# The gate z of the first layer, projected with channels as rows

## The chip, the core and the metric

The kernel runs on one core of a Trainium2 chip. The metric is the device time of one execution in microseconds (us); lower is better. Five engines work from queues of their own, each in its own order: TensorE (PE, with its weight loads listed as PEld), VectorE (DVE), ScalarE (ACT), GpSimd (POOL) and SyncE (SP, which issues most transfers). An instruction waits at the head of its queue until its semaphores are there, and everything behind it on that engine waits too.

## What is computed

Two mixers follow each other over 1024 tokens of 1024 channels: a gated DeltaNet layer, then a Mamba-2 layer. The change lies in the first one. Cut to what matters:

```python
proj = hid @ w_in
qkv, z, b_raw, a_raw = jnp.split(proj, [...], axis=-1)
qkv = jax.nn.silu(_causal_conv(qkv, conv_w))
...                                   # 8 key heads, 16 value heads of 128
o = _chunk_gated_delta_rule(q, k, v, g, beta).astype(hid.dtype)
o = _rmsnorm(o, norm_w) * jax.nn.silu(z.reshape(b, t, GDN_H_V, GDN_DV))
return o.reshape(b, t, GDN_V_W) @ w_out
```

z is a projection of 2048 channels, silu(z) a factor for each element of the normalised output, and the product goes into the output projection.

## The kernel before

The first layer runs in 8 groups g, each of one key head with its two value heads. In a group, q, k and the two v heads are projected by `proj_halves` (L160): the weights of 128 channels stand in the array, and 512 tokens stream past. One *half* is 24 matmuls 128x512 (L170, L171, L172: three products of high and low parts of a float32, over 8 slices of the 1024 input channels) into one `ps_proj` bank, of which there are two. Each half is drained by the convolution: ACT reads the bank (L202, L205), DVE adds three taps (L209), ACT and DVE make the silu (L189, L190). The weights come by a transfer to `wr`, a cast on ACT to `wh` (L86) and a subtraction on DVE to `wl` (L87); `wh` and `wl` have three slots each, each for half of the input channels.

The gate z is made the other way round, by `z_chunk` (L224): for each 128-token chunk n the tokens are the weights of the array, and 256 columns (two heads) of the z weights stream past, 24 matmuls 128x256 (L232, L233, L234). The result has tokens as rows. ACT takes a tanh (L238), DVE makes the silu (L239). The weights of z (`zh`, `zl`, one set of tiles) are loaded for a whole group by `load_zw` (L215).

The scan of a group walks over the 8 chunks. A *chain step* is a loop through three engines: `KS` on PE (L631, state S times k), `vpp` on DVE (L634), `NV` on PE (L639), `p` on ACT (L642), `dS` on PE (L648), S on DVE (L651, L654), and then the next KS. Beside it, `prep` makes the next chunk's operands (L609 to L620), and `output` makes the chunk's result o (L666, L668), its scale `so` (ACT and POOL, L680 to L683) and yn = o x so x z on DVE (L685). Two steps later `store` turns yn with two transposes on PE (L66) into `ps_tr`, ACT copies that to `yg` with the norm's weight (L695), and SP sends it off to y0d.

The order of the work: the program emits, in each of 8 slots of a group, one piece of scan S, one piece of I (the block inverse of the next group, L466) and one of J (a half of q, v, k of later groups), with z of the chunk inside the scan's piece. The scheduler then orders each engine's queue, the chain going with priority. At the very start the DVE queue is laid out by hand by a string, one letter a piece: Z (load of z's weights), I (inverse of group 0, 31 pairs of L490 and L492 among it), Y (three early z chunks), J, Q.

## Time and profile before

| | us |
|---|---|
| median of 3 runs | 1994.41 (1993.93 to 1996.84) |
| profiled execution: its own time is its span | 1993.9 |
| PE busy | 1918.5 (96%) |
| PE weight loads busy | 1644.6 (82%) |
| DVE busy | 1397.9 (70%) |
| ACT busy | 1120.4 (56%) |
| POOL busy | 420.5 (21%) |

Busy times are sums over the span; shares are of the span. Matmuls overlap, and their ends are modelled, so that two starts in a row tell more than a busy time. In a timeline a row's first number is its start in us from the span's beginning, its second how long it was listed as busy, and a bracket at its end names the idle time ahead of it on its engine and what ended it. x2 or x4 behind a row are so many matmuls that go as one row there: each product of float32 operands in the scan is listed as two.

### The profile page before, as it was taken

To read this page: it belongs to the slowest core of one execution; us is meant where nothing else is said; L and a number is where in the kernel's file an instruction comes from. 1 tells how busy PE (TensorE), PEld (TensorE's weight loads), DVE (VectorE), ACT (ScalarE), POOL (GpSimd) and SP (SyncE) were. 2 spreads that over 40 slices of the span, in tenths; PEclk is the share of its full clock that TensorE was granted. 3 is DMA by queue.
4 is the path that set the end of the run, shared out by engine and by line. 5 is a ranking of instruction groups with operands and counts; after the bars stand their busy time and mean duration, and the time that the engine had idled before them with its cause. 6 is when DMAs were issued, how large, how long until landed. Compare 5 with 4: busy or idle time off the path is not lost.

```text
span 1993.9 us, 36924 instructions
## 1 busy us (share of the span) xinstructions
PE 1918.5 (96%) x13086; PEld 1644.6 (82%) x13086; DVE 1397.9 (70%) x3330; ACT 1120.4 (56%) x3058; POOL 420.5 (21%) x818
## 2 busy tenths in 40 slices
PE   7997999899999999999999999999999999999998
PEld 5776888788888888897878788888888888897886
DVE  6797686777678776844355678778787877878433
ACT  5645656575656656564343466666665656566332
POOL 1201211212122212100000032333333233332000
PEclk9997999999999999999999999999999999999999
DMA  4421423232232423225474232222231322246754
GB/s 140 117 54 51 96 56 83 67 78 75 50 96 47 106 49 104 56 90 164 142 222 140 64 89 82 64 72 78 80 83 55 90 59 70 79 123 184 214 170 141
DMA packets 284796, 193.42 MB, mean 97 GB/s; under 512 B 65425, under 2 KB 246338, under 8 KB 284610
## 3 DMA queue, kind: packets, MB, share of 16 engines
q1 hardware_dynamic: 284610, 191.05, 34.1%
q8 instruction: 103, 1.69, 0.4%
q14 instruction: 83, 0.68, 0.1%
HBM read 159.34 MB, written 31.65 MB: 96 GB/s over the span
## 4 chain that ended last, share of the span: by engine, by line
PE 71%; DMA 8%; DVE 8%; ACT 4%; POOL 2%; issue 2%; SPq 1%; POOLq 0%; DVEq 0%; ACTq 0%
PE ps_proj L170 9%; PE ps_proj L172 8%; PE ps_proj L171 8%; PE ps_proj L352 5%; PE ps_proj L354 5%; PE ps_proj L353 5%; PE ps_proj L232 5%; PE ps_proj L233 5%; PE ps_proj L234 5%; PE ps_tr L66 2%; DMA X<-xd 2%; DVE acc L209 2%; PE ps_sc L910 2%; PE ps_pt L66 2%; PE ps_sc L639 1%
## 5 line engine op out<-in xcount | busy, mean ns | idle before, releaser
L170 PE MATMUL ps_proj<-hid_h,wh 128*128 128x512 f32 x1024 | 413.4, 404 | 5.2 <-ACT acc L205 4.0
L172 PE MATMUL ps_proj<-hid_h,wl 128*128 128x512 f32 x1024 | 404.0, 395 | 0.0
L171 PE MATMUL ps_proj<-hid_l,wh 128*128 128x512 f32 x1024 | 402.0, 393 | 0.0
L232 PE MATMUL ps_proj<-zh,hid_h 128*128 128x256 f32 x1024 | 297.5, 291 | 1.1 <-DVE z L239 1.0
L234 PE MATMUL ps_proj<-zh,hid_l 128*128 128x256 f32 x1024 | 294.7, 288 | 0.0
L233 PE MATMUL ps_proj<-zl,hid_h 128*128 128x256 f32 x1024 | 291.8, 285 | 0.0
L170 PEld LDWEIGHTS ps_proj<-hid_h,wh 128*128 128x128 f32 x1024 | 192.4, 188 | 44.7 <-ACT acc L205 4.9
L172 PEld LDWEIGHTS ps_proj<-hid_h,wl 128*128 128x128 f32 x1024 | 192.3, 188 | 40.6
L171 PEld LDWEIGHTS ps_proj<-hid_l,wh 128*128 128x128 f32 x1024 | 192.7, 188 | 34.8
L352 PE MATMUL ps_proj<-woh,yh 128*128 128x512 f32 x512 | 205.5, 402 | 6.4 <-ACT yh L86 4.0
L353 PE MATMUL ps_proj<-wol,yh 128*128 128x512 f32 x512 | 203.5, 400 | 0.7 <-DVE wol L87 0.7
L354 PE MATMUL ps_proj<-woh,yl 128*128 128x512 f32 x512 | 202.5, 398 | 1.2 <-DVE yl L87 1.0
L232 PEld LDWEIGHTS ps_proj<-zh,hid_h 128*128 128x128 f32 x1024 | 194.9, 190 | 6.5 <-DVE z L239 2.6
L233 PEld LDWEIGHTS ps_proj<-zl,hid_h 128*128 128x128 f32 x1024 | 195.0, 190 | 3.3
L234 PEld LDWEIGHTS ps_proj<-zh,hid_l 128*128 128x128 f32 x1024 | 195.0, 190 | 0.3
L209 DVE SCALAR_TENSOR_TENSOR acc<-raw,cw_ssd,acc 128x512 f32<-128x512 f32 x192 | 150.6, 785 | 19.4 <-ACT acc L207 17.2
L86 ACT CAST yh<-yr 128x512 fp32r<-128x512 f32 x128 | 79.0, 619 | 140.7 <-PE ps_proj L353 86.2
L87 DVE TENSOR_TENSOR yl<-yr,yh 128x512 fp32r<-128x512 f32 x128 | 88.7, 694 | 95.5 <-ACT yh L86 93.8
L209 DVE SCALAR_TENSOR_TENSOR acc<-raw,cw_gdn,acc 128x512 f32<-128x512 f32 x192 | 145.4, 758 | 12.6 <-ACT acc L205 11.2
L322 POOL TENSOR_SCALAR_AFFINE_SELECT gcrow<-gcrow 128x512 f32<-128x512 f32 x128 | 92.6, 727 | 257.8 <-DMA gcrow<-gcr_g 143.5
L873 ACT ACTIVATE lt<-gcrow,neggc_s 128x128 f32<-128x128 f32 x256 | 93.0, 397 | 78.2 <-DVE mt L875 67.5
L681 POOL TENSOR_SCALAR so<-so,cq 128x2 f32<-128x2 f32 x64 | 27.6, 431 | 464.0 <-ACT yn L680 464.0
(252 smaller groups left out, 4142.0 us busy)
## 6 DMA issues: line engine op xcount, KB each, us to landing
wr<-in_gdn_w_in_dram SPq DMA_DIRECT2D x96, 256.0 KB, 3.0
wr<-in_ssd_w_in_dram SPq DMA_DIRECT2D x96, 256.0 KB, 2.9
gcrow<-gcr_g SPq DMA_DIRECT2D x64, 256.0 KB, 3.6
yr<-y0d SPq DMA_DIRECT2D x64, 256.0 KB, 3.5
gcrow<-gcr_s SPq DMA_DIRECT2D x64, 256.0 KB, 3.7
yr<-y1d SPq DMA_DIRECT2D x64, 256.0 KB, 3.6
y0d<-yg SPq DMA_DIRECT2D x64, 128.0 KB, 1.9
wr<-in_gdn_w_out_dram SPq DMA_DIRECT2D x32, 256.0 KB, 3.5
```

Source lines behind the costliest of these rows:

```text
L170: nc.tensor.matmul(pt[0:nco], hi[:, j, 0:nco], xh[:, j, :], start=first, stop=False)
L171: nc.tensor.matmul(pt[0:nco], hi[:, j, 0:nco], xl[:, j, :], start=False, stop=False)
L172: nc.tensor.matmul(pt[0:nco], lo[:, j, 0:nco], xh[:, j, :], start=False, stop=last)
L209: nc.vector.scalar_tensor_tensor(out=acc, in0=raw[:, k:k + 512], scalar=cw[:, k * 32 + ti:k * 32 + ti + 1], in1=acc, op0=ALU.mult, op1=ALU ...
L232: nc.tensor.matmul(pt, xh, zh[:, k, :], start=k == 0, stop=False)
L233: nc.tensor.matmul(pt, xh, zl[:, k, :], start=False, stop=False)
L234: nc.tensor.matmul(pt, xl, zh[:, k, :], start=False, stop=k == KT - 1)
L322: nc.gpsimd.affine_select(out=t, in_=t, pattern=[[0, 4], [1, P]], compare_op=ALU.is_ge, fill=-1e30, base=0, channel_multiplier=-1)
L352: nc.tensor.matmul(pt, yh[:, j, :], hi[:, j, :], start=first, stop=False)
L353: nc.tensor.matmul(pt, yh[:, j, :], lo[:, j, :], start=False, stop=False)
L354: nc.tensor.matmul(pt, yl[:, j, :], hi[:, j, :], start=False, stop=last)
L873: nc.scalar.activation(lt, rows[h][:, n % 4, :], AF.Exp, bias=Gs["neggc"][:, h0 + h, n:n + 1])
```

## The change

z of the first layer is now made by `proj_halves` too, one head at a time: channels as rows, 512 tokens as columns, 24 matmuls 128x512 a half, four halves a group. A half is drained by a tanh on ACT (L593 of the changed kernel) and the silu on DVE (L594) into `zT`, of which four buffers hold two groups' worth. The scan no longer has z: yn is o x so alone, and `store` multiplies by zT and the norm's weight in one DVE instruction (L703) that reads the transposed tile from PSUM, in place of ACT's copy. `load_zw` and `z_chunk` are gone from this layer.

The four z halves of a group are the first of its J pieces. A group has 12 J pieces then instead of 8, and a table deals them out: slots 0 to 7 of a group take (2, 2, 1, 2, 1, 2, 1, 1), group 0 one each, and the last group (2, 1, 1). The string at the start loses Z and Y and gets K (a half of group 0's z) four times.

```diff
-        def z_weights(g):
-            GS[g]["zw"] = load_zw(gw, gw_in, 4096 + g * 256, ("zh", "zl"), 1)
+        def z_halves(g, h):
+            zT = GS[g].setdefault("zT", [gw.tile([P, 2, 512], F32, tag="zT", name="zT", bufs=4) for _ in range(2)])
+            def consume(th, pt):
+                tz = cv.tile([P, 512], F32, tag="th", name="tz")
+                nc.scalar.activation(tz, pt, AF.Tanh, scale=0.5)
+                nc.vector.scalar_tensor_tensor(out=zT[th][:, h, :], in0=tz, scalar=1.0, in1=pt, op0=ALU.add,
+                                               op1=ALU.mult)
+            yield from proj_halves(gw_in, 4096 + (2 * g + h) * P, hid, consume)
...
-                    nc.vector.scalar_tensor_tensor(out=yn[:, hs[h]], in0=o[:, hs[h]], scalar=so[:, h:h + 1],
-                                                   in1=z[:, hs[h]], op0=ALU.mult, op1=ALU.mult)
+                    nc.vector.tensor_scalar(out=yn[:, hs[h]], in0=o[:, hs[h]], scalar1=so[:, h:h + 1], scalar2=None,
+                                            op0=ALU.mult)
...
-                nc.scalar.activation(yg.rearrange("p h t -> p (h t)"), pt[:, 0:256], AF.Copy, scale=gnw_half)
+                nc.vector.scalar_tensor_tensor(out=yg, in0=pt[:, 0:256].rearrange("p (h t) -> p h t", t=P),
+                                               scalar=gnw_half, in1=E["zT"][n // 4][:, :, (n % 4) * P:(n % 4 + 1) * P],
+                                               op0=ALU.mult, op1=ALU.mult)
...
-                elif g < 7:
-                    Z[n] = z_chunk(gw, hid, E["zw"], n)
...
-            js = []
+            js = [z_halves(g, 0), z_halves(g, 1)]
...
-            for c in "ZIYIYIYIIJQQQII":
+            for c in "IKIKIKIKIJQQQII":
...
-                        next(J, None)
+                        for _ in range(((1,) * 8, (2, 2, 1, 2, 1, 2, 1, 1), (2, 1, 1, 0, 0, 0, 0, 0))[(g > 0) + (g > 6)][slot]):
+                            next(J, None)
```

How PE's queue stands in the middle of a scan. Of the kernel before, in group 2, two chain steps in a row; ps_sc is the scan's bank, `ps_proj_4730` a half of J, `ps_proj_4793` a chunk of z (24 matmuls, of which the first three are shown):

```order
L648 MATMUL ps_sc_4532<-p_4529,ktok_4347 128x128 x2
L666 MATMUL ps_sc_4538<-S_4244,qT_2900 128x256
L668 MATMUL ps_sc_4538<-p_4391,att_4201 128x128 x2
L172 MATMUL ps_proj_4730<-hid_h11_98,wl_4578 128x512
L170 MATMUL ps_proj_4730<-hid_h11_98,wh_4577 128x512
L171 MATMUL ps_proj_4730<-hid_l11_102,wh_4577 128x512
L172 MATMUL ps_proj_4730<-hid_h11_98,wl_4578 128x512
L631 MATMUL ps_sc_4683<-S_4535,kT_2477 128x256
L639 MATMUL ps_sc_4683<-vpp_4685,nte_2656 128x128 x2
L232 MATMUL ps_proj_4793<-zh_4156,hid_h01_96 128x256
L233 MATMUL ps_proj_4793<-zl_4157,hid_h01_96 128x256
L234 MATMUL ps_proj_4793<-zh_4156,hid_l01_100 128x256
```

Behind KS and NV (L631, L639) stands a whole z chunk before the step's dS, and behind dS the tail of a half before the next KS.

Of the changed kernel, the middle of a scan (group 3); KS is L640, NV L648, dS L657 there:

```order
L172 MATMUL ps_proj_6114<-hid_h11_98,wl_6065 128x512
L640 MATMUL ps_sc_5650<-S_5538,kT_3680 128x256
L66 MATMUL ps_tr_5623<-ident_73,yn_5550 128x128
L66 MATMUL ps_tr_5639<-ident_73,kT_3681 128x128
L618 MATMUL ps_tr_5639<-qT_4290,kT_3681 128x128
L66 MATMUL ps_tr_5623<-ident_73,yn_5550 128x128
L648 MATMUL ps_sc_5650<-vpp_5652,nte_3830 128x128 x2
L657 MATMUL ps_sc_5660<-p_5657,ktok_5517 128x128 x2
L674 MATMUL ps_sc_5666<-S_5404,qT_4289 128x256
L676 MATMUL ps_sc_5666<-p_5532,att_5386 128x128 x2
L640 MATMUL ps_sc_5817<-S_5663,kT_3681 128x256
L648 MATMUL ps_sc_5817<-vpp_5819,nte_3830 128x128 x2
```

From one KS to the next, and on to its NV, no row of `ps_proj` stands; the step behind it reads the same, and the next row of `ps_proj` comes after a third KS.

DVE's queue at the start, before, among the pairs L490 and L492 of the first inverse (Dt is the block that they fill; z0 is the first early chunk):

```order
L239 SCALAR_TENSOR_TENSOR z0_1050<-tz_1076,ps_proj_1051 128x256
L490 TENSOR_TENSOR tm_1079<-Dt_1013,X_1009 128x78
L492 TENSOR_REDUCE Dt_1013<-tm_1079 128x6
L490 TENSOR_TENSOR tm_1082<-Dt_1013,X_1009 128x98
L492 TENSOR_REDUCE Dt_1013<-tm_1082 128x7
```

The z weights were split ahead of the pairs there. After the change, at the same place:

```order
L492 TENSOR_REDUCE Dt_995<-tm_1029 128x6
L87 TENSOR_TENSOR wl_1037<-wr_1034,wh_1036 128x512
L87 TENSOR_TENSOR wl_1043<-wr_1040,wh_1042 128x512
L594 SCALAR_TENSOR_TENSOR zT_1032<-tz_1071,ps_proj_1046 128x512
L490 TENSOR_TENSOR tm_1074<-Dt_995,X_991 128x78
L492 TENSOR_REDUCE Dt_995<-tm_1074 128x6
```

Both weight splits of z's first head and its first silu stand between two pairs, and the same three stand again further down for the second head.

## Rows read from the trace of the kernel before

**Rows 1.** The page, busy time, share of the span and instructions of each engine.

```profile
PE 1918.5 (96%) x13086; PEld 1644.6 (82%) x13086; DVE 1397.9 (70%) x3330; ACT 1120.4 (56%) x3058; POOL 420.5 (21%) x818
```

**Rows 2.** A 125-us stretch: busy PE, PEld, DVE, ACT, POOL; granted clock; transfers' share; GB/s.

```profile
500.00:625.00 125.00, 120.62 (x913) 105.94 (x913) 92.59 (x249) 76.96 (x243) 24.61 (x47) 0.99 0.26 65
```

**Rows 3.** Groups by form: busy us, mean ns, idle before and its releasers; projections.

```profile
L170 PE MATMUL ps_proj<-hid_h,wh 128*128 128x512 f32 x1024 | 413.4, 404 | 5.2 <-ACT acc L205 4.0 <-DVE z L239 0.9
L232 PEld LDWEIGHTS ps_proj<-zh,hid_h 128*128 128x128 f32 x1024 | 194.9, 190 | 6.5 <-DVE z L239 2.6 <-ACT acc L205 0.2
```

**Rows 4.** Timeline of PE, the middle of a scan: start us, us, instruction.

```profile
500.04 0.40 PE L170 MATMUL ps_proj<-hid_h,wh 128*128 128x512 f32 x1
...
503.24 0.40 PE L172 MATMUL ps_proj<-hid_h,wl 128*128 128x512 f32 x1
...
503.71 0.59 PE L170 MATMUL ps_proj<-hid_h,wh 128*128 128x512 f32 x1
504.14 0.40 PE L171 MATMUL ps_proj<-hid_l,wh 128*128 128x512 f32 x1
...
505.07 0.37 PE L232 MATMUL ps_proj<-zh,hid_h 128*128 128x256 f32 x1
505.27 0.28 PE L233 MATMUL ps_proj<-zl,hid_h 128*128 128x256 f32 x1
...
507.29 0.27 PE L232 MATMUL ps_proj<-zh,hid_h 128*128 128x256 f32 x1
```

**Rows 5.** Groups by form, whole kernel: two matmuls of the chain step.

```profile
L639 PE MATMUL ps_sc<-vpp,nte 128*128 128x128 f32 x224 | 37.5, 291 | 9.9 <-DVE vpp L634 9.9
L631 PE MATMUL ps_sc<-S,kT 128*128 128x256 f32 x112 | 36.1, 404 | 6.9 <-DVE S L654 4.9 <-DVE S L651 1.9
```

**Rows 6.** Timeline of PE in group 0, where chain steps have no projection between them.

```profile
171.00 1.22 PE L631 MATMUL ps_sc<-S,kT 128*128 128x256 f32 x2
...
177.94 0.76 PE L631 MATMUL ps_sc<-S,kT 128*128 128x256 f32 x2
179.40 0.71 PE L639 MATMUL ps_sc<-vpp,nte 128*128 128x128 f32 x4 [0.70 <-DVE vpp L634]
180.71 0.74 PE L648 MATMUL ps_sc<-p,ktok 128*128 128x128 f32 x4 [0.60 <-ACT p L642]
...
182.78 0.70 PE L631 MATMUL ps_sc<-S,kT 128*128 128x256 f32 x2
186.16 0.71 PE L639 MATMUL ps_sc<-vpp,nte 128*128 128x128 f32 x4 [2.68 <-DVE vpp L634]
```

**Rows 7.** Busy time by stretches of 10 us there, columns as in Rows 2.

```profile
170.00:180.00 10.00, 8.43 (x32) 6.44 (x31) 7.66 (x25) 5.08 (x19) 1.92 (x4) 0.59 0.04 13
180.00:190.00 10.00, 6.72 (x49) 5.80 (x48) 9.64 (x27) 6.43 (x26) 1.93 (x4) 1.00 0.09 27
```

**Rows 8.** Groups by form: what drains z and the output, and nearest forms.

```profile
L239 DVE SCALAR_TENSOR_TENSOR z<-tz,ps_proj 128x256 f32<-128x256 f32 x128 | 52.8, 413 | 23.7 <-ACT tz L238 23.2
L190 DVE SCALAR_TENSOR_TENSOR acc<-th,acc 128x512 f32<-128x512 f32 x64 | 44.6, 697 | 8.0 <-ACT th L189 7.1
L695 ACT ACTIVATE yg<-ps_tr,gnw_half 128x256 f32<-128x256 f32 x64 | 31.2, 487 | 7.9 <-PE ps_tr L66 7.9
L620 DVE TENSOR_TENSOR att<-ps_tr,lt 128x256 f32<-128x256 f32 x64 | 26.8, 419 | 16.4 <-PE ps_tr L609 7.7 <-ACT lt L618 5.3 <-ACT ktok L613 3.1
```

**Rows 9.** Groups by form: the cast and split of projection weights.

```profile
L87 DVE TENSOR_TENSOR wl<-wr,wh 128x512 fp32r<-128x512 f32 x128 | 89.0, 696 | 49.9 <-ACT wh L86 47.8 <-PE ps_proj L171 1.5
L86 ACT CAST wh<-wr 128x512 fp32r<-128x512 f32 x128 | 78.9, 617 | 58.9 <-PE ps_proj L171 46.8 <-DMA wr<-in_gdn_w_in_dram 6.6 <-PE ps_proj L172 2.1
```

**Rows 10.** Timeline at the start: DVE's last pair; PE's first product of the inverse.

```profile
128.10 0.68 DVE L492 TENSOR_REDUCE Dt<-tm 128x16 f32<-128x512 f32 x1
142.78 0.21 PE L509 MATMUL ps_pt<-Ds,nte 32*32 32x32 f32 x1
```

**Rows 11.** Busy time in 10 us of the start, columns as in Rows 2.

```profile
110.00:120.00 10.00, 10.00 (x46) 8.29 (x45) 8.64 (x18) 3.41 (x6) 0.19 (x1) 1.00 0.20 53
```

More of the change, by code (lines that the diff above doesn't have):

```diff
@@ L597, in scan @@
             rows = {}
-            A, C, Z, Y = {}, {}, {}, {}
+            A, C, Y = {}, {}, {}
             def prep(n):
@@ L661, in output @@
                 p, S = C.pop(n)
-                z = Z.pop(n)
                 po = ps_sc()
@@ L699, in scan @@
             prep(0)
-            if g == 7:
-                zt = [gw.tile([P, 2, 256], F32, tag=t, name="z7", bufs=b)
-                      for t, b in (("kT", 4), ("kT", 4), ("vs", 6), ("vs", 6))]
             for n in range(NT):
@@ L707, in scan @@
                     prep(n + 1)
-                if n in E.get("Zp", ()):
-                    Z[n] = E["Zp"].pop(n)
-                elif g < 7:
-                    Z[n] = z_chunk(gw, hid, E["zw"], n)
-                elif n < 4:
-                    for m in (2 * n, 2 * n + 1):
-                        Z[m] = z_chunk(gw, hid, E["zw"], m, zt[m // 2][:, m % 2, :])
                 with tc.high_priority(60):
@@ L736, in js_of @@
         def js_of(g):
-            js = []
+            js = [z_halves(g, 0), z_halves(g, 1)]
             if g < 7:
-                js = [q_halves(g + 1), v_halves(g + 1, 0), v_halves(g + 1, 1)]
+                js += [q_halves(g + 1), v_halves(g + 1, 0), v_halves(g + 1, 1)]
             if g < 6:
@@ L742, in js_of @@
             return chain_halves(*js)
-        def once(f, *a):
-            f(*a)
-            yield
-        def early_z():
-            Zp = GS[0]["Zp"] = {}
-            zt = gw.tile([P, 2, 256], F32, tag="vs", name="z0", bufs=6)
-            for n in range(3):
-                Zp[n] = z_chunk(gw, hid, GS[0]["zw"], n, zt[:, n, :] if n < 2 else None)
-                yield
         J = chain_halves(q_halves(0), v_halves(0, 0), v_halves(0, 1), k_halves(1))
-        todo = {"J": J, "P": k_products(0), "I": inverse(0), "Q": k_products(1), "Z": once(z_weights, 0), "K": js_of(0),
-                "Y": early_z()}
+        todo = {"J": J, "P": k_products(0), "I": inverse(0), "Q": k_products(1), "K": js_of(0)}
         for c in "PPPPJJJJJJJ":
@@ L788, in hybrid_trunk @@
             next(S, None)
-            if g < 7:
-                z_weights(g + 1)
     bpool = ctx.enter_context(tc.tile_pool(name="bpool", bufs=2))
```

## The prediction

> **What bounds the kernel now.** I read the page's busy shares first: PE is listed busy for 96% of the span and DVE for 70% [rows 1]. A modelled PE busy time proves nothing by itself, so I went to a stretch of the first layer, where PE has 120.62 us of 125, DVE 92.59 and ACT 76.96, at a granted clock of 0.99 [rows 2], and then to the starts of single matmuls. They follow each other without a hole: a 512-wide one every 0.229 us (14 steps from 500.04 to 503.24), a 256-wide one every 0.119 us (17 steps from 505.27 to 507.29) [rows 4]. So PE is the bound there, by the rate at which columns stream and not by a wait. The waits say the same: the chain step's KS and NV were waited for 6.9 and 9.9 us in the whole kernel, 16.8 us over 56 steps (each KS is listed as two), or 0.3 us a step [rows 5]. That is little because projection matmuls stand in PE's queue between the chain's parts and cover the way through DVE and ACT. Where they don't, in group 0, a step takes 4.84 us (KS at 177.94, the next at 182.78), and PE stands between KS and NV and between NV and dS [rows 6], at the full clock [rows 7]. The reader should see two prices there: what a projection matmul costs PE, and what a chain step costs when it is alone.
>
> **The form of the product.** The first layer loses 64 chunks x 24 = 1536 matmuls of 256 columns and gains 32 halves x 24 = 768 of 512: as many columns, half as many instructions. By the starts of [rows 4], 1536 x 0.1188 = 182.5 us become 768 x 0.2286 = 175.6 us, a gain of 6.9 us, on the path, since PE is the bound. The Trainium skill ("TensorE: Matmul & The Clock Gate", Back-to-back issue gap) gives an isolated warm matmul its columns over 2.4 GHz and about 2.5 ns more. By it two 256-wide ones would cost only 2.5 ns over a 512-wide one, the gain would be 1.9 us, and the sum below 5 us higher; the starts here show some 9 ns instead.
>
> **Fewer changes of kind.** The first projection matmul behind scan work costs more than its pitch: 503.71 to 504.14 is 0.20 us over, 505.07 to 505.27 is 0.08 over [rows 4]; between them I take 0.1. Counted along PE's queue in the first layer, such changes fall from 252 to 195, so 57 x 0.1 = 5.7 us are gained, with 4.6 and 11.4 as ends.
>
> **Work on DVE and ACT.** DVE loses half of L239's 52.8 us (26.4) and gains 32 x 0.697 = 22.3 us of silu in the form of L190; the new L703 reads PSUM and writes 256 columns, nearest to L620's 0.419 us, at most L695's 0.487: 64 x 0.42 to 0.49 = 27 to 31 us [rows 8]. yn loses one operand, for little. DVE gets some 25 us more over the eight groups; ACT loses the 31.2 us of L695 and gains nothing of that size. Beside a PE that fills 120 of 125 us, with DVE at 92.6 [rows 2], 3 us a group are hidden, and I put them at zero. Without that cover, where DVE is what the chain waits for, one L703 a bare step counts: at most 14 x 0.5 = 7 us. The transfer to y0d leaves in the same place on SP, behind yg as before, and z's weights now come in 256-KB pieces of the same ring; zero.
>
> **The start.** DVE's queue now has z's weight splits and silus between the pairs of the first inverse. Only one slot of `wh` and `wl` is free there, so the second split (wl_1043) stands until the first weights have been used, 24 x 0.229 = 5.5 us and a cast of 0.62 [rows 9], less the first split's own 0.70; then the silu stands for some 14 matmuls more, 3.2 us. Two heads make about 17 us in which DVE stands with the pairs queued behind it. Before, DVE was 8.64 us of 10 busy in that stretch [rows 11], so about 4 us of standing and of early z work were there already: the last pair, at 128.10 before, and with it the inverse on PE, at 142.78 [rows 10], come some 13 us later, 19 if PE's own waiting for the splits is added. Against that, PE has 11 halves of 5.49 us behind it when the first scan begins, 60 us, where it had 6 halves and 5 chunks of 2.85 us, 47 us: 13 us of projection that needs no place later. The difference is 0 to 6 us; I take +3. Ends: -6, if the pairs are delayed less than DVE's count says, and +13, if what is done early has no use later.
>
> **Cover that leaves the scan.** This is the large term. Before, z's chunk stood inside every chain step, and J's half beside it. Now z is the front of the J pieces, and the table gives two halves to slots 0, 1, 3 and 5. PE's queue in the middle of each scan from group 1 on shows two chain steps in a row with no projection matmul from KS to KS, 14 steps in all (in the last group they stand at the front of the scan); before, the same stretch had a chunk or a half in every step but for single legs. What such a step costs PE is read in group 0 [rows 6]. The profile's own idle there is 0.70 + 0.60 = 1.3 us a step. By starts it is more: KS to NV is 1.46 us, of which its two matmuls need 2 x 0.119 = 0.24; NV to dS is 1.31 us, of which four narrower ones need at most 0.48; that leaves 1.22 + 0.83 = 2.05 us. The next step there waited 2.68 us for vpp alone, 3.3 with p, because DVE (9.64 of 10 us, [rows 7]) had other work queued. Less the 0.3 us that a step loses already, the term is 14 x (2.05 - 0.3) = 25 us, with ends of 14 x 1.0 = 14 and 14 x 3.0 = 42. I take the middle one: starts are measured, the profile's busy ends are modelled, and the double slots ahead leave DVE drained or backlogged about as in the first of these steps. What is late next is DVE: in the bare steps its own work a step comes near PE's. A further price is open: the granted clock averages 0.59 in the ten us after the long hole of group 0, where a step took 6.94 us (171.00 to 177.94) [rows 6, 7]. A bare pair is short, and at 180 to 190 the clock stayed at 1.00 [rows 7], so I take zero, with two such slow steps as an end: 4 us.
>
> **The sum.** -6.9 - 5.7 + 3 + 25 = +15.4 us on the profiled 1993.9, or 2009.3; the median of the runs is 0.5 above the profiled one, so 2010. The ends: -6.9 - 11.4 - 6 + 14 = -10 at the low, -6.9 - 4.6 + 13 + 42 + 7 + 4 = +55 at the high; that all ends fall on one side is unlikely, and the case's own range is 1999 to 2036.
>
> **Rivals.**
> Faster, by the cover being paid back: PE is the bound, and its work falls by 12.6 us. If the double halves let DVE and ACT clear what they owe, the bare steps run on ready operands, and the waits that they show replace those that other steps had (16.8 us of the chain's, 5.2 at L170 [rows 3, 5]). The place is the two bare steps; it decides from an added idle below (12.6 - 3) / 14 = 0.7 us a step, half of the profile's own 1.3. At zero the time is 1993.9 - 9.6 + 0.5 = 1985, with 1980 if the start gains too. For it: the chain has priority, and nothing else is changed. Against it: the loop through DVE and ACT has a length of its own, which no backlog shortens. Chance 0.20.
>
> Level: the bare steps cost about 0.7 us more each, for instance because transposes and the inverse's products fall into them on the chip; gains and losses meet within 0.2% (4 us, about what a measurement of this kernel can tell from no change), 1994. Chance 0.11.
>
> DVE becomes the bound of each scan: its 25 us more don't hide, each bare step waits for 3.3 us as at 186.16 [rows 6], and the double halves bring six taps and two silus at once; 1993.9 - 9.6 + 42 + 25 = 2051, more likely half of the extra, 2039. For it: DVE is at 99% in places [rows 7]. Against it: 92.6 of 125 us on average [rows 2]. Chance 0.06.
>
> The weight loads are the bound: each matmul has a load of 0.190 us [rows 3], listed busy for 82% [rows 1], and 768 fewer would be worth 146 us, or 1848. Starts of 256-wide matmuls 0.119 us apart [rows 4] are closer than a load is long, so loads overlap and don't set the pace. The Trainium skill ("Perfetto Trace Analysis", Identifying the Most-Contended Engine) judges TensorE's headroom by the busy share of weight loads rather than of matmuls, which would make this the likely case; the pitch speaks against it. Chance 0.02.
>
> **How the numbers follow.** The forecast, slower by bare steps, has 0.61: 2010, in 1999 to 2036. With the 0.06 of the DVE case, slower by over 0.2% has 0.67; level has 0.11; the paid-back cover and the weight loads make faster 0.22. A range of 8 in 10 takes the forecast's own range, level, and most of the faster case: 1984 to 2036 leaves out the DVE case, the weight loads and the tails.
>
> **What would show it.** Right: 512-wide starts 0.229 us apart for z; KS and NV waiting clearly over 16.8 us in all, most of it for vpp, in two steps of each group at 2 us each; the first inverse on PE 13 to 19 us after 142.78; a group period some 3 us longer. Wrong: bare steps of 4.84 us with other work on PE in their gaps, or steps shorter than that; the start delayed by much more than 19 us, or not at all; waits of `ps_proj` on DVE, which would put DVE in the place of PE.

## The result

The changed kernel takes 2020.8 us (median of 4 runs, 2017.9 to 2024.1) against 1994.2 of the kernel before: 1.0128 times as long (95% interval 1.0113 to 1.0144), 26.6 us more. The page of its profiled execution:

```profile
span 2018.7 us, 35389 instructions
...
PE 1922.8 (95%) x12318; PEld 1609.4 (80%) x12318; DVE 1411.5 (70%) x3362; ACT 1096.4 (54%) x2962; POOL 408.6 (20%) x818
```

Against [rows 1], PE has 768 matmuls fewer and is listed busy 4 us longer, in a span 24.8 us longer. DVE has 13.6 us more work. The page alone doesn't tell where the time went. The chain's matmuls, grouped by form (busy, mean ns, idle before and its releaser), answer to [rows 5], and the two new DVE instructions to [rows 8]:

```profile
L648 PE MATMUL ps_sc<-vpp,nte 128*128 128x128 f32 x224 | 38.9, 297 | 19.8 <-DVE vpp L643 19.8
L657 PE MATMUL ps_sc<-p,ktok 128*128 128x128 f32 x224 | 42.7, 311 | 11.3 <-ACT p L651 11.0 <-ACT ktok L622 0.3
L640 PE MATMUL ps_sc<-S,kT 128*128 128x256 f32 x112 | 36.4, 408 | 5.7 <-DVE S L660 2.8 <-DVE S L663 2.7
...
L703 DVE SCALAR_TENSOR_TENSOR yg<-ps_tr,gnw_half,zT 128x256 f32<-128x256 f32 x64 | 30.7, 479 | 22.9 <-PE ps_tr L66 22.8
...
L594 DVE SCALAR_TENSOR_TENSOR zT<-tz,ps_proj 128x512 f32<-128x512 f32 x32 | 21.8, 682 | 14.3 <-ACT tz L593 14.3
```

NV waits twice as long for vpp (19.8 us against 9.9), and KS less than before (5.7 against 6.9). dS now waits 11.3 us, nearly all of it for p; it waited 2.1 us in the kernel before:

```profile
L648 PE MATMUL ps_sc<-p,ktok 128*128 128x128 f32 x224 | 38.3, 294 | 2.1 <-ACT p L642 2.1
```

L703 takes 0.479 us, near the upper of the two prices taken.

**Where the time went, by group.** I cut both traces at the first NV of each scan (before: 159.3, 234.1, 338.0 and so on; after: 184.0, 268.9, 369.6 ...), counted the projection matmuls in each piece, and took 0.2286 us for a 512-wide and 0.1188 for a 256-wide one off its length. What is left, called the remainder below, is the scan's own PE work and everything lost: idle time, changes of kind, a low clock. These windows, with the matmuls that write ps_proj, are of the kernel after (start, group 1, group 4; busy PE, PEld, DVE, ACT, granted clock, transfers' share, GB/s):

```profile
60.00:184.00 124.00, 95.92 (x383) 72.98 (x381) 2.73 (x4) 16.63 (x28) 0.92 0.28 74
268.90:369.60 100.70, 52.55 (x209) 38.25 (x209) 0.69 (x1) 10.40 (x17) 0.97 0.28 68
588.70:695.20 106.50, 69.91 (x284) 52.42 (x284) 2.04 (x3) 11.64 (x19) 0.98 0.29 72
```

Group 1 has 209 matmuls, 100.7 - 209 x 0.2286 = 52.9 us left; group 4 has 284 and 41.6. The whole first layer, in us of that remainder:

| stretch | before | after | more |
|---|---|---|---|
| 60 us to the first NV | 24.5 | 36.9 | 12.4 |
| group 0 | 48.4 | 49.2 | 0.8 |
| group 1 | 38.6 | 52.9 | 14.3 |
| groups 2 to 6 | 202.0 | 205.3 | 3.3 |
| group 7 to the end of the output projection | 42.7 | 43.5 | 0.8 |

The remainders grow by 31.6 us, and the projections shrink by 6.9 at these prices; together 24.7, against 24.8 between the two spans. This sum closes by its construction, so it places the loss but tests no price; and it is read from one profiled execution of each kernel. The loss sits at the start and in group 1, and the five groups in the middle lose little more than they did before.

**The start.** The waits of DVE there, of the kernel after, and its last pair:

```profile
109.37 0.69 DVE L87 TENSOR_TENSOR wl<-wr,wh 128x512 fp32r<-128x512 f32 x1 [7.42 <-ACT wh L86]
113.59 0.69 DVE L594 SCALAR_TENSOR_TENSOR zT<-tz,ps_proj 128x512 f32<-128x512 f32 x1 [3.53 <-ACT tz L593]
131.34 0.69 DVE L87 TENSOR_TENSOR wl<-wr,wh 128x512 fp32r<-128x512 f32 x1 [8.19 <-ACT wh L86]
135.54 0.69 DVE L594 SCALAR_TENSOR_TENSOR zT<-tz,ps_proj 128x512 f32<-128x512 f32 x1 [3.50 <-ACT tz L593]
...
148.38 0.69 DVE L492 TENSOR_REDUCE Dt<-tm 128x16 f32<-128x512 f32 x1
```

DVE stands 7.42 + 3.53 + 8.19 + 3.50 = 22.6 us, at the places foretold; the pairs end 20.3 us later than in [rows 10]. PE's first product of the inverse answers to the last of [rows 10], 25.1 us later:

```profile
167.85 0.21 PE L509 MATMUL ps_pt<-Ds,nte 32*32 32x32 f32 x1
```

Meanwhile the clock falls twice; windows of the start, all engines and then the granted clock, and the longest wait of PE next to each:

```profile
95.00:105.00 10.00, 4.84 (x17) 4.06 (x18) 6.10 (x18) 2.29 (x6) 0.10 (x1) 0.50 0.10 27
119.00:129.00 10.00, 6.27 (x16) 4.54 (x15) 3.88 (x10) 0.00 (x0) 0.00 (x0) 0.50 0.09 26
...
97.68 1.12 PE L66 MATMUL ps_pt<-ident,acc 128*128 128x128 f32 x4 [5.42 <-DVE acc L190]
...
123.21 0.79 PE L172 MATMUL ps_proj<-hid_h,wl 128*128 128x512 f32 x1 [3.73 <-DVE wl L87]
```

Both are at the lower level, 1.2 GHz. Only the second stands beside a wait for a split. At the first, PE waits for the drain of a half of q, k or v, before any weight of z has been split. In the kernel before, two early z chunks fill PE there until 97.7 us, and the same wait is 2.87 us. So part of the start's loss is no standstill of DVE, but cover that had stood ahead of it.

**The bare steps.** A bare step is a chain step without a projection matmul. Groups 2 to 6 have nine of the fourteen: one in group 2 and two in each of the others. Group 4, its two, PE's row (some rows between left out):

```profile
640.16 0.59 PE L640 MATMUL ps_sc<-S,kT 128*128 128x256 f32 x2
641.92 0.30 PE L66 MATMUL ps_tr<-ident,yn 128*128 128x128 f32 x1 [1.17 <-DVE yn L693]
...
643.03 0.71 PE L648 MATMUL ps_sc<-vpp,nte 128*128 128x128 f32 x4 [0.36 <-DVE vpp L643]
644.20 0.93 PE L657 MATMUL ps_sc<-p,ktok 128*128 128x128 f32 x4 [0.46 <-ACT p L651]
...
646.62 1.06 PE L640 MATMUL ps_sc<-S,kT 128*128 128x256 f32 x2
649.07 0.71 PE L648 MATMUL ps_sc<-vpp,nte 128*128 128x128 f32 x4 [1.38 <-DVE vpp L643]
650.24 0.75 PE L657 MATMUL ps_sc<-p,ktok 128*128 128x128 f32 x4 [0.46 <-ACT p L651]
650.82 0.60 PE L674 MATMUL ps_sc<-S,qT 128*128 128x256 f32 x2
651.25 0.61 PE L676 MATMUL ps_sc<-p,att 128*128 128x128 f32 x4
```

The brackets alone are 3.8 us for the two, 1.9 a step; in the step of [rows 6] they were 1.3, and the price taken by starts was 2.05. A row of L657 that starts at 644.20 and is listed 0.93 us, against 0.75 at 650.24, shows something else: the clock is at half there.

```profile
640.00:650.00 10.00, 6.41 (x29) 4.47 (x27) 8.83 (x22) 4.67 (x17) 2.22 (x4) 0.83 0.25 68
```

A stretch of 3.4 us at half the clock lies at this place in each of groups 2 to 6 (it begins at 433.0, 542.2, 644.6, 757.3 and 863.1 us). So the bare steps cost what was forecast and a little more, and yet the remainders of these groups grow by 3.3 us in all. Two things pay for it. Groups 2 to 6 whole, of the kernel before and then of the changed one:

```profile
338.00:866.80 528.80, 506.58 (x4018) 447.00 (x4017) 390.52 (x1074) 323.98 (x1001) 104.08 (x195) 0.98 0.29 74
369.60:909.40 539.80, 517.94 (x3570) 432.73 (x3569) 402.49 (x1101) 315.25 (x946) 91.04 (x193) 0.98 0.29 76
```

PE is not listed busy for 22.2 us before and 21.9 us after: the waits in the bare steps replace others. By the lines of these stretches NV and dS wait 13.0 us where they waited 4.6, while KS falls from 4.9 to 2.0, the transposes of yn from 6.9 to 4.8, and the first matmul of a half from 2.9 to nothing. And the kernel before has three stretches at half the clock in these groups, 17.1 us in all, as much as the five of the changed kernel, though it has no bare step there. So neither waiting nor the clock grew.

### The profile page after: what moved, and what is told of

Same layout as the page of the kernel before. It is cut to its first block, busy times and chain, and to the rows that moved or that the text cites. A ratio compares the mean times of both kernels' runs of the same rounds, so it can differ in the third digit from the quotient of the medians.

```text
span 2018.7 us, 35389 instructions
## 1 busy us (share of the span) xinstructions
PE 1922.8 (95%) x12318; PEld 1609.4 (80%) x12318; DVE 1411.5 (70%) x3362; ACT 1096.4 (54%) x2962; POOL 408.6 (20%) x818
## 4 chain that ended last, share of the span: by engine, by line
PE 67%; DVE 12%; DMA 6%; issue 4%; ACT 3%; POOL 2%; SPq 0%; POOLq 0%; DVEq 0%; ACTq 0%
PE ps_proj L170 10%; PE ps_proj L172 9%; PE ps_proj L171 9%; PE ps_proj L354 5%; PE ps_proj L352 5%; PE ps_proj L353 5%; PE ps_proj L233 2%; PE ps_proj L232 2%; PE ps_proj L234 2%; DVE acc L209 2%; PE ps_tr L66 2%; DVE tm L490 2%; DVE Dt L492 2%; PE ps_pt L66 2%; PE ps_sc L897 2%
## 5 line engine op out<-in xcount | busy, mean ns | idle before, releaser
L170 PE MATMUL ps_proj<-hid_h,wh 128*128 128x512 f32 x1280 | 517.0, 404 | 5.5 <-DVE zT L594 3.0
L172 PE MATMUL ps_proj<-hid_h,wl 128*128 128x512 f32 x1280 | 508.4, 398 | 3.7 <-DVE wl L87 3.7
L171 PE MATMUL ps_proj<-hid_l,wh 128*128 128x512 f32 x1280 | 507.2, 396 | 0.0
L87 DVE TENSOR_TENSOR wl<-wr,wh 128x512 fp32r<-128x512 f32 x160 | 113.2, 708 | 94.8 <-ACT wh L86 87.2
L234 PE MATMUL ps_proj<-zh,hid_l 128*128 128x256 f32 x512 | 146.9, 287 | 0.0
L86 ACT CAST wh<-wr 128x512 fp32r<-128x512 f32 x160 | 98.4, 616 | 87.4 <-PE ps_proj L171 83.8
L232 PE MATMUL ps_proj<-zh,hid_h 128*128 128x256 f32 x512 | 145.4, 284 | 0.0
L233 PE MATMUL ps_proj<-zl,hid_h 128*128 128x256 f32 x512 | 144.2, 282 | 0.0
L189 ACT ACTIVATE th<-acc 128x512 f32<-128x512 f32 x128 | 80.9, 632 | 93.0 <-DVE acc L209 88.7
L352 PEld LDWEIGHTS ps_proj<-woh,yh 128*128 128x128 f32 x512 | 96.6, 189 | 28.3 <-ACT yh L86 5.3
```

The lines of the kernel that those rows point to most:

```text
L86: nc.scalar.copy(hi, src)
L87: nc.vector.tensor_tensor(out=lo, in0=src, in1=hi.bitcast(F32), op=ALU.subtract)
L170: nc.tensor.matmul(pt[0:nco], hi[:, j, 0:nco], xh[:, j, :], start=first, stop=False)
L171: nc.tensor.matmul(pt[0:nco], hi[:, j, 0:nco], xl[:, j, :], start=False, stop=False)
L172: nc.tensor.matmul(pt[0:nco], lo[:, j, 0:nco], xh[:, j, :], start=False, stop=last)
L232: nc.tensor.matmul(pt, xh, zh[:, k, :], start=k == 0, stop=False)
```

## The experiments

Each kernel was timed beside the kernel before on the same chip. That kernel's own median moved by up to 0.3% from one occasion to another, also on one chip (1995.2 and 2000.9 us), so kernels of different occasions are compared by their ratio to it. What is said of clocks, waits and remainders is read from one profiled execution of each.

| kernel | us | before beside it | ratio (95%) |
|---|---|---|---|
| changed | 2020.8 | 1994.2 | 1.0128 (1.0113 to 1.0144) |
| e1_late | 2006.0 | 1995.2 | 1.0053 (1.0035 to 1.0071) |
| e2_late_z2 | 2009.5 | 1995.2 | 1.0065 (1.0041 to 1.0089) |
| e3_own | 2017.0 | 1995.2 | 1.0110 (1.0085 to 1.0136) |
| e4_before_z4 | 1994.3 | 1995.2 | 1.0002 (0.9989 to 1.0015) |
| e5_preload | 2005.1 | 1995.7 | 1.0057 (1.0037 to 1.0077) |
| e6_act | 2003.7 | 1995.7 | 1.0039 (1.0020 to 1.0057) |
| e7_256 | 1978.5 | 1995.7 | 0.9925 (0.9898 to 0.9952) |
| e8_after256 | 2007.5 | 2000.9 | 1.0036 (1.0020 to 1.0052) |
| e9_two_late | 1987.1 | 2000.9 | 0.9929 (0.9913 to 0.9944) |
| e10_four_early | 1981.5 | 2000.9 | 0.9907 (0.9889 to 0.9926) |
| e11_out256 | 2000.9 | 1998.0 | 1.0020 (1.0008 to 1.0031) |
| e12_two_thirds | 2010.7 | 1998.0 | 1.0063 (1.0049 to 1.0078) |

**e1: the start string.**

```diff
-            for c in "IKIKIKIKIJQQQII":
+            for c in "IIIIIJQQQIIKKKK":
```

> The changed kernel with one string altered: the four z halves of group 0 stand behind the pairs of the first inverse, its products and k's second half on VectorE's queue, not between the pairs. In TensorE's queue they then fall into the first scan, whose steps were bare, and group 1 has its full share of filler. Two bare chain steps stay in each later scan, 16 in all. Theory A (most of the 26 us is lost at the start and, for want of filler, in group 1: 12 and 14 us by the segments of the two traces; the bare steps of the later groups cost about 1 us a group): 1995 to 2000 us. Theory B (the prediction's weights: 25 us in the bare steps of all groups, 3 at the start): 2014 to 2019 us.

It came out at 1.0053, some 15 us below the changed kernel: between the theories. Group 1 is mended (remainder 41.5 us instead of 52.9) and the first scan has filler (37.1 instead of 49.2). But the start itself now loses more, 46.9 us: while DVE works through the pairs, PE has nothing at all. Ten microseconds of it, all engines and the clock:

```profile
110.00:120.00 10.00, 0.00 (x0) 0.00 (x0) 9.42 (x18) 0.00 (x0) 0.00 (x0) 0.50 0.00 0
```

So z's early halves did feed PE at the start; taking them away moves the loss there.

**e2: zT with two buffers, 9 bare steps instead of 16.**

```diff
-            zT = GS[g].setdefault("zT", [gw.tile([P, 2, 512], F32, tag="zT", name="zT", bufs=4) for _ in range(2)])
+            zT = GS[g].setdefault("zT", [gw.tile([P, 2, 512], F32, tag="zT", name="zT", bufs=2) for _ in range(2)])
```

> As e1_late, and zT with two buffers instead of four, so that the z halves of a group cannot run ahead into the scan before: TensorE's queue then has 9 bare steps instead of 16. Theory A: 1 to 4 us below e1_late, since a bare step of a later group costs about half a microsecond. Theory B: 7 bare steps x 1.75 us = 12 us below e1_late.

No gain: 1.0065 against 1.0053, within the intervals. Both theories' 'fewer bare steps are faster' fell. One bare step is left in each group. In the profiled execution, the slowest of its five, the clock is at half for 6.8 us behind it in groups 2 to 5 and for 3.4 in group 6, where e1 had 3.4 or none. One of them, all engines and the clock:

```profile
419.80:426.60 6.80, 6.31 (x24) 5.55 (x25) 5.50 (x13) 3.04 (x11) 1.28 (x2) 0.50 0.26 41
```

Groups 2 to 6 keep 213.4 us of remainder, e1 203.2; the difference is half of the 20.5 us more that e2 has at half the clock there. The number of bare steps is not the measure; what PE's clock does behind them counts too.

**e3: slots of their own for group 0's z weights** (zT has three buffers there, to make room).

```diff
+            if own is not None:
+                hi = own.tile([P, 4, P], F32R, tag="ownh", name="wh", bufs=2)
+                lo = own.tile([P, 4, P], F32R, tag="ownl", name="wl", bufs=2)
...
-            yield from proj_halves(gw_in, 4096 + (2 * g + h) * P, hid, consume)
+            yield from proj_halves(gw_in, 4096 + (2 * g + h) * P, hid, consume, own=gw if g == 0 else None)
```

> The changed kernel with its start, but the z weights of group 0 have slots of their own (and zT three buffers, to make room), so that the second split does not wait for a slot. If the standstill on VectorE comes from the slot, the last pair and the first scan come 8 to 12 us earlier than in the changed kernel; group 1 stays short of filler. Theory A with the slot as the cause of the start: 2009 to 2014 us. Theory B: 2017 to 2020 us. If the standstill is the wait of the silus for whole halves on TensorE instead: no earlier scan, 2019 to 2022 us.

1.0110, some 4 us less than the changed kernel by the ratios, with overlapping intervals. DVE's three waits of the start, from the fastest of its four runs:

```profile
104.64 0.69 DVE L87 TENSOR_TENSOR wl<-wr,wh 128x512 fp32r<-128x512 f32 x1 [3.32 <-ACT wh L86]
109.99 0.69 DVE L598 SCALAR_TENSOR_TENSOR zT<-tz,ps_proj 128x512 f32<-128x512 f32 x1 [4.65 <-ACT tz L597]
129.82 0.69 DVE L598 SCALAR_TENSOR_TENSOR zT<-tz,ps_proj 128x512 f32<-128x512 f32 x1 [9.66 <-ACT tz L597]
```

The splits wait less, the silus more: 17.6 us of standing instead of 22.6, and the first scan begins 5.6 us earlier, not 8 to 12. A slot alone helps little, since the silu stands in DVE's queue right behind its split and waits for the half.

**e4: the kernel before, with four buffers for z's chunks.**

```diff
-            z = pool.tile([P, 256], F32, tag="z", name="z", bufs=2)
+            z = pool.tile([P, 256], F32, tag="z", name="z", bufs=zb)
...
-                    Z[n] = z_chunk(gw, hid, E["zw"], n)
+                    Z[n] = z_chunk(gw, hid, E["zw"], n, zb=4)
...
```

> The kernel before with one number altered: the chunks of z have four buffers instead of two. They can then run ahead of the scan, and TensorE's queue has one bare step in each scan from group 1 on, and fewer projection matmuls in the steps around it. If bare steps cost 1.75 us each, as the prediction has it: 1994 + 12 = 2006 us. If they cost about half a microsecond: 1996 to 1999 us. If running ahead costs nothing: 1994 us.

No change (1.0002). PE's queue has its bare step in each scan from group 1 to group 6, but groups 2 to 6 keep 201.7 us of remainder (202.0 before). That doesn't make a bare step free: the five of these groups wait 2.2 to 3.2 us each. Seven microseconds with the one of group 5, all engines and the clock:

```profile
725.20:732.20 7.00, 3.84 (x23) 2.72 (x22) 5.21 (x12) 3.60 (x13) 0.97 (x2) 1.00 0.34 71
```

But the clock is at half in only one of these groups, for 3.4 us, where the kernel before has 17.1 us of it. The timed runs show the same: granted clocks of 0.989 to 0.994, against 0.984 to 0.989 of the kernel before beside it. The clock lost over the span is 17 us on average against 27, so up to 10 us were got back there, near the 12 us that the bare steps were priced at. So e4 leaves the price of a bare step open; why the clock stays up is not shown.

**e5: the first head's weights split ahead of the pairs, two halves between the pairs, two behind.**

```diff
-            for c in "IKIKIKIKIJQQQII":
+            for c in "AIKIKIIIJQQQIIKK":
```

Piece A loads and splits the first z head's weights into slots of their own (zT has three buffers, as in e3).

> The changed kernel with another start: the weights of group 0's first z head are cast and split ahead of the pairs into slots of their own (zT has three buffers to make room), only that head's two z halves stand between the pairs, one piece of pairs ahead of each, and the second head's two come behind the inverse, into the first scan. The pairs then need not wait for a cast, and TensorE has as much to do beside them as in the kernel before. Two bare steps stay in each scan. Theory C (the whole loss is the start: VectorE's standstills, TensorE at half the clock behind the holes, and filler used ahead that group 1 lacks; bare steps of later groups are paid back by shorter waits elsewhere): the first scan begins within 6 us of the kernel before, 1988 to 1997 us. Theory B (bare steps cost 1.75 us each): 2008 us or more. If the silus on VectorE still stand for their halves: about 2005 us.

1.0057: like e1. DVE no longer stands among the pairs, and they end at 119.86 + 0.69 us, 8 us earlier than in [rows 10]. But PE's two halves last only to 110 us; it idles for 14 us and is at half the clock for 27.3 (110 to 120 us, all engines and the clock):

```profile
110.00:120.00 10.00, 0.52 (x2) 0.08 (x1) 9.42 (x18) 0.00 (x0) 0.00 (x0) 0.62 0.00 0
```

The remainder of the start is 36.8 us, as bad as that of the changed kernel, from the other side: there PE waited for DVE's queue, here DVE is early and PE has no work. Groups 2 to 6 keep 207.0, 5 us more than in the kernel before; start, group 0 and group 1 keep 123.6, 12 more. So the scan begins early enough, as theory C asked, and its 1988 to 1997 us are missed all the same: a start that only frees DVE leaves PE bare. The 2005 us of the third case came true by number and not by its cause, for no silu stands among the pairs.

**e6: yg on ScalarE again, z left out of the output.**

```diff
-                nc.vector.scalar_tensor_tensor(out=yg, in0=pt[:, 0:256].rearrange("p (h t) -> p h t", t=P),
-                                               scalar=gnw_half, in1=E["zT"][n // 4][:, :, (n % 4) * P:(n % 4 + 1) * P],
-                                               op0=ALU.mult, op1=ALU.mult)
+                nc.scalar.activation(yg.rearrange("p h t -> p (h t)"), pt[:, 0:256], AF.Copy, scale=gnw_half)
```

> As e5_preload, but yg is again made by ScalarE's copy with the norm's weight, and the factor z is left out of the output; z is projected and its silu made as there. It tells what the 64 multiplications that read PSUM cost on VectorE. If VectorE's added work is hidden, as the prediction has it: within 4 us of e5_preload. If VectorE sets the pace of the full chain steps: 64 x 0.48 = 31 us less work there, 8 to 20 us below e5_preload.

1.5 us below e5 by the medians, with overlapping intervals. To take 31 us of work and the wait for the transposes from DVE, and to give ACT its copy back, changes nothing that can be measured: the multiplication out of PSUM is hidden.

**e7: z's matmuls in two 256-wide pieces, on the base of e5.**

```diff
-                    nc.tensor.matmul(pt[0:nco], hi[:, j, 0:nco], xh[:, j, :], start=first, stop=False)
-                    nc.tensor.matmul(pt[0:nco], hi[:, j, 0:nco], xl[:, j, :], start=False, stop=False)
-                    nc.tensor.matmul(pt[0:nco], lo[:, j, 0:nco], xh[:, j, :], start=False, stop=last)
+                    for wt, x_, a, b in ((hi, xh, first, False), (hi, xl, False, False), (lo, xh, False, last)):
+                        for c in range(parts):
+                            cs = slice(c * (512 // parts), (c + 1) * (512 // parts))
+                            nc.tensor.matmul(pt[0:nco, cs], wt[:, j, 0:nco], x_[:, j, cs], start=a and c == 0,
+                                             stop=b and c == parts - 1)
```

> As e5_preload, but each 512-wide matmul of the first layer's z is issued as two 256-wide ones with the same weights, 1536 in place of 768. The prediction's term for the form is 6.9 us, by starts 0.1188 and 0.2286 us apart: 5 to 9 us above e5_preload by it, 2 us by an issue gap of 2.5 ns. TensorE's queue is ordered somewhat differently (one bare step a scan at its end instead of two in its middle), which by theory C is worth little and by theory B some 10 us less.

The surprise: with the dearer form it is 27 us faster than e5, and faster than the kernel before (0.9925). The instructions are the same but for the split; what differs is the order that the scheduler makes of them. It deals z out in other portions, and no step of groups 2 to 6 is left without a projection matmul: from one KS to the next they hold 88, 69, 57, 60, 10, 40, 34 and 26 in most groups, of either width, where e5 has 67, 63, 60, 0, 0, 45, 22 and 27. Those groups keep 185.9 us of remainder, 21 less than e5, and the clock doesn't fall in any of them:

```profile
375.00:500.00 125.00, 122.14 (x910) 106.39 (x910) 98.98 (x277) 73.78 (x222) 21.05 (x48) 1.00 0.27 69
500.00:625.00 125.00, 120.24 (x906) 104.70 (x904) 100.28 (x265) 72.93 (x219) 21.20 (x44) 1.00 0.29 73
```

Against [rows 2], DVE is 8 us busier in 125 us and PE is no busier. What the order saves can be read in groups 2 to 6 whole, of e5 and then of e7:

```profile
359.20:895.20 536.00, 513.37 (x3547) 428.87 (x3546) 398.36 (x1098) 311.92 (x944) 89.96 (x195) 0.98 0.28 75
349.00:866.70 517.70, 505.41 (x4053) 446.23 (x4052) 395.33 (x1091) 309.64 (x940) 94.78 (x195) 1.00 0.29 76
```

PE is not listed busy for 22.6 us in e5 and 12.3 in e7, and e5 has 17.1 us at half the clock, worth up to 8.5. The two make nearly 19 of the 21 us.

**e8: the same split, with the changed kernel's own start.**

> The changed kernel with its own start, and each 512-wide matmul of the first layer's z issued as two 256-wide ones, as in e7_256: TensorE's queue is then ordered as there from group 3 on. e7_256 came out 27 us below e5_preload, though its form costs some 7 us more. If that gain is the order of the later groups alone, it adds to the changed kernel whatever its start: 2020.8 - 27 = 1994, 1989 to 1999 us. If it needed the other start too: 2003 us or more.

1.0036, 0.92% below the changed kernel: 18 us, between the two cases and not the 27 foretold. Groups 2 to 6 keep 193.3 us of remainder (205.3 in the changed kernel), but the start (36.3) is as it was, and group 1 (47.8) is only 5 us better. The order of the later groups is a gain by itself, and what is left between this kernel and e7 is mostly ahead of them: the start and groups 0 and 1 keep 135.2 us here and 116.5 in e7.

**e9 and e10: two other starts on the base of e7.**

```diff
-            for c in "AIKIKIIIJQQQIIKK":
+            for c in "AIKIKIIIJQQQII":
```

e9 also has the table (2, 2, 1, 1, 1, 1, 1, 1) for group 0; e10 has the string "AIKIKIJIKIKQQQII".

> As e7_256, but the second z head of group 0 is no part of the string: its two halves are the first pieces of the group's slots (2, 2, 1, 1, 1, 1, 1, 1). TensorE's queue then has four more halves ahead of the first inverse, where it stood 13.8 us in e7_256 and fell to half the clock for 24 us, and the first scan is bare again, as in the kernel before. Start and first scan together took 24.8 + 48.5 = 73.3 us beside the projections in the kernel before, 78.1 in e7_256. If feeding TensorE at the start is worth more than the hole it leaves: 1970 to 1977 us. If it is only moved: 1977 to 1981. If group 1 then lacks filler, as in the changed kernel: 1985 us or more.

> As e7_256, but all four z halves of group 0 come ahead of the second half of the pairs, as in the changed kernel, with the first head's weights split ahead and k's second half before the second head, so that no split waits long for a slot. VectorE has more to do ahead of the last pair. If the early halves as such cost the start (pairs late, first scan bare): 6 to 14 us above e9_two_late. If only the standstills for slots did: within 4 us of e9_two_late.

e9 is at 0.9929 and e10 at 0.9907, with e7 at 0.9925; the intervals overlap. e9 has only moved its loss, as its second case had it. e10 is not slower than e9 but 5.6 us faster by the medians. So early halves as such cost nothing that shows here. In e10 all four stand early, as in the changed kernel, and the start keeps 25.3 us (before 24.5, changed 36.9). Its DVE has one wait of note there, for the second head's first half:

```profile
129.89 0.69 DVE L600 SCALAR_TENSOR_TENSOR zT<-tz,ps_proj 128x512 f32<-128x512 f32 x1 [6.65 <-ACT tz L599]
```

The form isn't the reason, for e8 has it too and keeps 36.3 us at the start. So the cost of the start is not that z is early. It is that splits, halves and silus wait for each other one at a time in DVE's queue. By its interval e10 beats both kernels, 0.9889 to 0.9926 of the kernel before; e7 and e9 do so too.

**e11: the form by itself, in the output projections of the kernel before.**

```diff
-                        nc.tensor.matmul(pt, yh[:, j, :], hi[:, j, :], start=first, stop=False)
-                        nc.tensor.matmul(pt, yh[:, j, :], lo[:, j, :], start=False, stop=False)
-                        nc.tensor.matmul(pt, yl[:, j, :], hi[:, j, :], start=False, stop=last)
+                        for wt, x_, a, b in ((yh, hi, first, False), (yh, lo, False, False), (yl, hi, False, last)):
+                            for c in range(2):
+                                cs = slice(c * 256, (c + 1) * 256)
+                                nc.tensor.matmul(pt[:, cs], wt[:, j, :], x_[:, j, cs], start=a and c == 0, stop=b and c == 1)
```

> The kernel before with the 1536 matmuls of 512 columns of the two output projections issued as 3072 of 256 columns, where no chain runs beside them for most of the time. It measures the form by itself. By the starts of the trace of before (0.2376 for two of 256 against 0.2286 us for one of 512) 1536 x 9 ns = 14 us slower; by an issue gap of 2.5 ns 1536 x 2.5 = 4 us slower.

1.0020 (1.0008 to 1.0031), 4 us for 1536 pairs, or 2.6 ns a pair (1.0 to 4.0). The rows in 40 us of the last output projection, of the kernel before and then of e11:

```profile
1880.00:1920.00 40.00, 40.00 (x176) 32.56 (x175) 13.61 (x21) 10.74 (x20) 1.01 (x3) 1.00 0.49 147
```

```profile
1880.00:1920.00 40.00, 40.00 (x338) 40.00 (x337) 12.82 (x19) 10.02 (x18) 1.00 (x3) 1.00 0.50 147
```

176 matmuls of 512 columns against 338 of 256, 169 pairs: 0.2273 against 0.2367 us, the 9 ns of [rows 4] again. The starts are right where PE alone is the limit. In the profiled executions the second layer's output projection is 4.3 us longer from first to last matmul, 5.6 ns for each of its 768 pairs, and that of the first layer is 2.2 us shorter. There the form can't be read, for the kernel before has 6.8 us at half the clock in it and e11 none. The Trainium skill ("TensorE: Matmul & The Clock Gate", Back-to-back issue gap) has 2.5 ns; the time over both projections comes near it, the starts do not, and with that difference of the clock the time is no test.

**e12: two of three products split.**

```diff
-                        for c in range(parts):
+                        np_ = parts if wt is hi else 1
+                        for c in range(np_):
...
```

> As e10_four_early, but only two of the three products of the first layer's z (those with the high weights) are issued as two 256-wide matmuls; the third stays 512 wide, 256 matmuls fewer. The form gains 256 x 9 ns = 2.3 us. TensorE's queue has one step of each scan without any projection matmul (40 ahead of it), where e10_four_early has at least 10 in that step. If a bare step costs idle time and a stretch at half the clock, as in the changed kernel: 5 to 20 us above e10_four_early by its ratio to the kernel before. If it costs what a step with 10 matmuls does: 0 to 3 us below.

1.0063 against e10's 0.9907: 31 us slower, in the main for one step of each scan that went from 10 projection matmuls to none. That is more than the widest expectation. PE at that place in group 3 of e12, and the clock behind it:

```profile
522.53 0.61 PE L683 MATMUL ps_sc<-p,att 128*128 128x128 f32 x4
525.26 0.70 PE L647 MATMUL ps_sc<-S,kT 128*128 128x256 f32 x2 [2.12 <-DVE S L670]
527.25 1.22 PE L655 MATMUL ps_sc<-vpp,nte 128*128 128x128 f32 x4 [1.30 <-DVE vpp L650]
528.93 1.22 PE L664 MATMUL ps_sc<-p,ktok 128*128 128x128 f32 x4 [0.46 <-ACT p L658]
```

```profile
526.40:533.20 6.80, 5.49 (x21) 4.93 (x22) 4.10 (x11) 2.62 (x10) 1.11 (x2) 0.50 0.40 80
```

And e10 at the same place, where ten projection matmuls follow KS:

```profile
518.54 0.75 PE L663 MATMUL ps_sc<-p,ktok 128*128 128x128 f32 x4 [0.56 <-ACT p L657]
...
521.65 0.70 PE L646 MATMUL ps_sc<-S,kT 128*128 128x256 f32 x2 [1.48 <-DVE S L669]
...
523.11 0.48 PE L177 MATMUL ps_proj<-hid_h,wh 128*128 128x512 f32 x1
```

```profile
523.00:530.00 7.00, 7.00 (x36) 5.39 (x34) 4.87 (x10) 5.11 (x21) 1.98 (x4) 1.00 0.44 67
```

e12 waits 3.9 us there, and each of its groups 2 to 6 has 6.8 us at half the clock; e10 waits 2.0 and keeps the clock in all five. The clock of e12 falls at 526.4 us, after the first of its waits (2.12 us) and inside the second, so what had passed by then differs little from e10. There e12 keeps 211.0 us of remainder against 187.6, 4.7 a group; some 2 of it is idle time (PE is not listed busy for 23.8 us against 13.4), and up to 6.8 / 2 = 3.4 the clock. Of the remaining difference, groups 0 and 7 have 4 us each, with more half-clock time in group 0 (17.1 against 10.2 us).

## Why the prediction was right, and where its steps were not

The sign and the range held: 2010 us forecast in 1984 to 2036, 2020.8 measured. But the sum came near by luck: the nine bare steps of groups 2 to 6 were priced at 16 of its main term's 25 us and came to 3, while the start, priced at 3, came to 27 with the loss of group 1 behind it. By the prediction's own steps:

**The start** (+3 us, ends -6 and +13) is the term that was mis-sized most. DVE's standstills were named at their places, but they are 22.6 us, not 17, and the inverse is 25.1 us late, not 13 to 19. The first NV comes 24.7 us later with 12.3 us more of projection done from 60 us on, so the start costs 12 by its remainder. Two things were missing. First, PE fell to half its clock for 20.5 us there (4.9 before), half of it beside a wait for a drain, not a split. Second, what was done ahead had little use later: group 1, with 209 matmuls where e1 has 299, has three bare steps and loses 14.3 us more. The end of +13 named that second case, but only in place of the first; both came, 27 us with group 0's 0.8. That early work must empty group 1 is not shown: e10 has as much done before its first scan and keeps 43.3 us in group 1, and its order gives groups 0 and 1 the worth of 86 and 275 matmuls, where the changed kernel has 156 and 209.

**The cover that leaves the scan** (+25 us, ends 14 and 42) had its gross price about right and its comparison wrong. A bare step waits 1.9 us by its brackets. The 2.05 by starts was itself read a little high: it took 0.119 us for each of the two matmuls of KS, but a product of that form takes 0.43 us to the next start (650.82 to 651.25), so that the step of [rows 6] loses 1.9. What failed is the step 'less the 0.3 us that a step loses already'. [rows 5] count only waits that end in KS and NV. PE as a whole was not busy for 22.2 us in groups 2 to 6 of the kernel before, and it is so for 21.9 in the changed kernel: the cover that left some steps went to others, and took as much waiting from them. So these groups lost 3.3 us in all and not the 15.8 that their nine bare steps at 1.75 make. The clock, which the prediction had at zero, is level there too, at 17.1 us of half clock in both; that bare steps have such stretches beside them is offset by those that the kernel before had without bare steps. e4 agrees in the total, but there the clock paid, so it is no proof that bare steps are free. e7, e10 and e12 show that both kernels were far from what these groups can reach.

**The form** (-6.9 us): the pitches hold, as e11's rows show. What a kernel gains of it depends on whether PE is the limit where it stands, and was not measured in the changed kernel by itself.

**DVE's added work at zero**: right for L703, its largest piece, by e6.

**Fewer changes of kind** (-5.7 us) were not measured apart; they are in the remainders. In groups 2 to 6, where waits and clock are level, the remainders still grew by 3.3 us, so no gain of that size shows.

Of the rivals, 'the cover being paid back' was right for groups 2 to 6, to within 3.3 us, though its bare steps still wait, and lost by the start and group 1. DVE as the bound is not borne out by e6, nor the weight loads by e11, where they are listed busy for 40.00 of 40 us, against 32.56, and the pitch per column changes by 4%. The Trainium skill ("Perfetto Trace Analysis", Identifying the Most-Contended Engine) would read the first as an engine without headroom; the time moved by 0.2%.

**What stays open**: why PE waits less in e7's order was not followed from step to step, and no kernel had the 512-wide form in e7's order, which by the starts would be some 7 us faster still. e7 against e5 is thus a difference of order with the form's price against it, and nothing finer.

## What to carry to other kernels

Before a filler is taken out of a dependent chain, weigh it against what the old order already loses, counted over everything that the engine does in a whole group and not by the waits that the chain's own lines show. Work put into a hand-ordered queue of an in-order engine must be there when the queue comes to it: a split, a product and its drain that follow each other through three engines cost their whole round trip each time, and an instruction that comes early for its input holds everything behind it. And when an edit changes the number or length of instructions, compare the orders that the scheduler makes of it: here e7's order was worth 27 us, against a form that is some 7 us dearer by its starts.

## What the runs showed of the hardware

The granted clock falls to half in short stretches (3.4, 6.8, 10.2 us and longer), often next to holes in PE's work, but the holes look much alike. With 3.9 us of waits in e12's step it fell in five groups of five; with 2.2 to 3.2 us in e4's bare step in one of five; with 2.0 us in e10's step in none. The kernel before has 17.1 us at half the clock in groups 2 to 6 without a bare step. Where ten projection matmuls stand in the step, a group was 4.7 us shorter than without them, and the clock stayed up (e10, e12). In the kernel before the layer had 47.8 us at half the clock, in the changed one 61.4, in e10 30.7, in e12 71.7; so the clock is at most some 7 of the 25 us between the first two. That the idle time is the smaller part of a hole's price in e12 I had not expected; in e7 against e5 it is the larger.
